# A two-layer trunk on one core: x also loaded by columns, and the first FFN's norm moved behind its first two column chunks

## The chip, the core and the metric

The kernel runs on one NeuronCore of a Trainium2 chip. Its engines work side by side, each through its own list of instructions in order: TensorE (PE; its weight loads are listed as PEld), VectorE (DVE), ScalarE (ACT), GpSimd (POOL), and SyncE (SP), which here only issues DMA transfers. They wait for each other through semaphores. TensorE takes its operands from SBUF and writes to PSUM, which has eight banks of 128x512 float32.

The metric is the device time of one execution in microseconds. Before the change it is 1176.08 us, the median of three runs (1176.0 to 1176.14).

## What is computed

Two layers, each of three sub-layers on the same 256x1024 stream x: a SwiGLU FFN with half a step, a token mixer (windowed attention beside a gated spatial unit), and a second FFN. Cut to what matters here:

```python
def rms_norm(x, g):
    x32 = x.astype(jnp.float32)
    y = x32 * lax.rsqrt(jnp.mean(x32 * x32, axis=-1, keepdims=True) + RMS_EPS)
    return (y * g.astype(jnp.float32)).astype(x.dtype)

def swiglu(x, w1, w2):
    g, u = jnp.split(x @ w1, 2, axis=-1)
    return (jax.nn.silu(g) * u) @ w2

for l in range(DEPTH):                       # DEPTH = 2
    h = rms_norm(x, ffn1_pre_g[l])
    x = x + 0.5 * rms_norm(swiglu(h, ffn1_w1[l], ffn1_w2[l]), ffn1_post_g[l])
    h = rms_norm(x, mix_pre_g[l])
    z = h @ w_in[l]
    ...                                      # attention, spatial gating, merge
    x = x + rms_norm(merged @ w_out[l], mix_post_g[l])
    h = rms_norm(x, ffn2_pre_g[l])
    x = x + 0.5 * rms_norm(swiglu(h, ffn2_w1[l], ffn2_w2[l]), ffn2_post_g[l])
```

x is 256x1024 (SEQ x D_MODEL), w1 is 1024x5632 (gate and value, 2816 columns each), w2 is 2816x1024. The part that changes is the very first FFN. Since the norm multiplies each token's row by one number, `rms_norm(x, g) @ w` equals `((x*g) @ w)` with each token's result multiplied by that number: the product can be taken first and scaled later.

## The kernel before

**Numbers.** Each product is made of three: every float32 operand is split in a high part (rounded to fp32r by ACT) and a low part (the rest, by DVE), and high x high, high x low and low x high are added up in PSUM. So each weight that is loaded costs one ACT cast (`Stream.high`, L143) and one DVE subtraction (`Stream.lower`, L152), and so does each activation.

**The stream of weights.** `Stream` holds all weights in units of 128x1024 float32 (512 KB) in the order in which they are used. SP loads a unit to one of four raw buffers (`RAW`); the load of unit u+4 is issued when DVE has made the low part of unit u (`low`, `lower`). `st.upto(n)` writes the casts and subtractions of all units below n into the lists of ACT and DVE at that place of the program. After `st.slip = True` each subtraction stands one unit behind its cast.

**The first FFN, first part.** The first 512 gate and 512 value columns (`FA` = 4 chunks of 128 of each) are computed token-major: for each of the two token tiles, 128 tokens of x are the stationary operand and 512 columns of weights the moving one. This takes eight units, 96 matmuls of 128x512, in `units(0)` to `units(7)` (helper L289). In the opening the input isn't normed yet. x comes in by rows, TensorE turns it (`transpose4`, L254, sixteen 128x128 transposes) and its gain is put on the weights or on x; the scale of the norm is put on the result in `first.finish` (L363, L364).

**The norm.** ACT squares and sums the rows (L214), DVE makes the inverse roots (L222 to L237) and a diagonal matrix from them (L269), TensorE spreads them over all partitions with a product with ones (L276), ACT copies that to SBUF (L278). DVE then multiplies the turned x with it (`norm`, L1141 and L1144), ACT casts and DVE subtracts (`high0`, `low0`, L1038, L1041). The result is `xt`, with high and low parts side by side for each of the eight 128-feature blocks k.

**The first FFN, second part.** The other 18 chunks of 128 gate and 128 value columns are computed feature-major in `FFN.middle`, chunks c = 4 to 21: the weights are stationary and `xt` moves. For one chunk `feature_pairs` (L319) issues 14 wide matmuls (512 columns: high and low part of x at once), 16 narrow ones (256 columns, low weights) and the two wide ones that were held back, gate and value each in a PSUM bank of its own. Then ACT copies (L680), DVE adds (L681), ACT takes the silu (L683), DVE multiplies gate by value (L684); then `st.upto` puts the casts and subtractions of two further units there, and the chunk's result is split for the second product (L206, L207). In the program `st.upto(8 + AHEAD)`, which covers the weights up to unit 14, and `first.finish` stand ahead of chunk 4's evacuation.

**What sets the order.** Everything is written out by hand; no scheduler moves an instruction. Each engine works through its list in the order of the program text, and the tile framework adds the waits. After the first FFN the kernel goes on through `project`, `Mix` and the others, which the change doesn't touch.

Of the kernel before, what the change touches and what calls it, by code (L numbers as in the profile page):

```python
# [54 lines left out]
WARM = (11, 6)  # L55
# [8 lines left out]
def trunk(ctx: ExitStack, tc: tile.TileContext, a: dict, out: bass.AP):  # L64
# [35 lines left out]
    class Stream:  # L100
        def __init__(self):
            self.src, self.where = [], []
            self.raw, self.split = {}, {}
            self.loaded = self.ready = 0
            self.free = RING
            self.rest = None
            self.slip = False
            self.gain = {}
# [14 lines left out]
        def first(self):  # L123

            self.raw[0] = new(rawp, [P, 1024], "raw")
            both = new(m8, [P, 2, 1024], "m8", F32R)
            self.split[0] = both[:, 0, :], both[:, 1, :]
            self.loaded = self.ready = 1
            for b in halves():
                nc.sync.dma_start(self.raw[0][:, b], self.src[0][:, b])  # L130
                yield
            for i in range(2):
                self.high(0, (i,))
                yield
                self.lower(0, (i,))
                yield
            del self.raw[0]
            self.load(1 + RAW)

        def high(self, u, which=(0, 1)):  # L140
            h = self.split[u][0]
            if u not in self.gain:
                nc.scalar.copy(h, self.raw[u])  # L143
                return
            for i in which:
                b = halves()[i]
                nc.scalar.activation(h[:, b], self.raw[u][:, b], AF.Copy, scale=self.gain[u][i])

        def lower(self, u, which=(0, 1)):
            h, lo = self.split[u]  # L150
            if u not in self.gain:
                nc.vector.tensor_tensor(out=lo, in0=self.raw[u], in1=f(h), op=ALU.subtract)  # L152
                return
            for i in which:
                b = halves()[i]
                nc.vector.scalar_tensor_tensor(out=lo[:, b], in0=self.raw[u][:, b], scalar=self.gain[u][i],
                                               in1=f(h[:, b]), op0=ALU.mult, op1=ALU.subtract)
# [25 lines left out]
        def low(self):  # L183

            if self.rest is not None:
                u = self.rest
                self.rest = None
                self.lower(u)
                del self.raw[u]
                self.load(u + 1 + RAW)  # L190
# [81 lines left out]
    def spread(dg):  # L272
# [4 lines left out]
        rb = new(t2, [P, n, P], "t2")  # L277
# [33 lines left out]
    def feature_pairs(os, us, both):  # L311
# [3 lines left out]
        wide = [[(o, st[u][0], flat(both[:, k]), k) for k in range(KD)] for o, u in zip(os, us)]  # L315
        narrow = [(o[:, 0:S], st[u][1], both[:, k, 0, :], k) for o, u in zip(os, us) for k in range(KD)]
# [334 lines left out]
    class FFN:  # L651
        def __init__(self, l, i, early=()):
            self.l, self.i = l, i
            w1, w2 = a[f"ffn{i}_w1"][l], a[f"ffn{i}_w2"][l]
            self.first = FirstFFN(l, i, early)
# [12 lines left out]
        def middle(self, xt, xth, xtl, turn1, early):  # L668
            for _ in range(2):
                self.into.append((new(m8, [P, 8, S], "m8", F32R), new(m8, [P, 8, S], "m8", F32R)))  # L670
            for c in range(FA, FC):
                o = [bank(), bank()]
                us = self.cols[(c - FA) * 2:(c - FA) * 2 + 2]
                feature_pairs(o, us, xt)
# [4 lines left out]
                for half in range(2):  # L679
                    nc.scalar.copy(y[:, half, :], o[half][:, S:2 * S])  # L680
                    nc.vector.tensor_tensor(out=y[:, half, :], in0=o[half][:, 0:S], in1=y[:, half, :], op=ALU.add)  # L681
                    if half == 0:
# [4 lines left out]
                split(hh, hl, s[:, S:2 * S])  # L687
                if c == FA + 2:
# [308 lines left out]
    def load_x(t, h):  # L997
        nc.sync.dma_start(xs[t][:, halves()[h]], a["x"][rows_of(t), halves()[h]])


    load_x(0, 0)
    begin = st.first()
    next(begin)
    load_x(1, 0)
    next(begin)
    st.load(2)
    load_x(0, 1)
    load_x(1, 1)
    st.load(RAW)

    for u in (0, 1, 4, 5):
        st.gain[u] = [g0[:, k:k + 1] for k in (u % 4 * 2, u % 4 * 2 + 1)]
# [15 lines left out]


    first = subs[0].first  # L1030
    xu = new(n8, [P, KD, S], "n8", F32R), new(n8, [P, KD, S], "n8", F32R)
    xg = [new(t4, [P, KD, P], "t4") for _ in range(NT)]

    def quarter0(t, h):
        return slice(None), slice(h * 4, h * 4 + 4), rows_of(t)

    def high0(x, t, h, src):
        nc.scalar.copy(x[0][quarter0(t, h)], src)  # L1038

    def low0(x, t, h, src):  # L1040
        nc.vector.tensor_tensor(out=x[1][quarter0(t, h)], in0=src, in1=f(x[0][quarter0(t, h)]), op=ALU.subtract)  # L1041

    one = []
    for t in range(NT):
        first.begin(t)
        one.append(first.steps(t, *xu)[3])

    def some(u, t, which):

        for k, i in which:  # L1050
            one[t](u // 4, u % 4 * 2 + k, (i,))
# [4 lines left out]
    def units(u):  # L1056

        for which in (SOON, LATE):
            for t in range(NT):
                some(u, t, which)  # L1060

    def warm(n):

        for _ in range(n):
            nc.tensor.transpose(cold[:, 0:P], ident, ident)  # L1065

    cold = bank()
# [3 lines left out]
    warm(WARM[0])  # L1071
    turned, src0 = {}, {}
    parts = [new(tiny2, [P, 2], "parts") for _ in range(NT)]

    def turn0(t, h):
# [170 lines left out]
```

## Time and profile before

| what | value |
|---|---|
| median of three runs | 1176.08 us (1176.0 to 1176.14) |
| the profiled execution: its time, its span | 1175.91 us, 1174.0 us |
| busy: PE, DVE, ACT, POOL | 1164.8, 842.6, 675.4, 58.9 us |
| instructions on PE | 6293 |
| HBM read over the span | 218.65 MB, 187 GB/s |

The time of an execution holds 1.9 us more than its span, which runs from the first instruction to the last. "Busy" counts an engine's instructions from start to end; matmuls overlap each other, so a lone 128x512 matmul is listed with 0.39 us while a row of them advances by some 0.23 us each. In a timeline row the first number is the start in us, the second the time from the first start to the last end of the merged instructions (xN), and a bracket tells how long the engine had been idle and what ended that.

### The profile page before, as it was taken

To read this page: it belongs to the slowest core of one execution; us is meant where nothing else is said; L and a number is where in the kernel's file an instruction comes from. 1 tells how busy PE (TensorE), PEld (TensorE's weight loads), DVE (VectorE), ACT (ScalarE), POOL (GpSimd) and SP (SyncE) were. 2 spreads that over 40 slices of the span, in tenths; PEclk is the share of its full clock that TensorE was granted. 3 is DMA by queue.
4 is the path that set the end of the run, shared out by engine and by line. 5 is a ranking of instruction groups with operands and counts; after the bars stand their busy time and mean duration, and the time that the engine had idled before them with its cause. 6 is when DMAs were issued, how large, how long until landed. Compare 5 with 4: busy or idle time off the path is not lost.

```text
span 1174.0 us, 16947 instructions
## 1 busy us (share of the span) xinstructions
PE 1164.8 (99%) x6293; PEld 1006.9 (86%) x6293; DVE 842.6 (72%) x1430; ACT 675.4 (58%) x1147; POOL 58.9 (5%) x43
## 2 busy tenths in 40 slices
PE   9999999999999999999999999999999999999997
PEld 7888888999888888888888888889988888888886
DVE  6767758877787867766676677589778787676752
ACT  6656644657775456555455665455577754555551
POOL 0000000001131000000000000000021220000000
PEclk9999999999999999999999999999999999999999
DMA  7576673645457346557635657745544662565560
GB/s 249 182 255 230 219 250 141 203 168 175 140 175 241 137 142 215 183 198 266 216 108 193 224 193 240 230 141 183 182 169 137 210 225 81 179 200 198 198 210 37
DMA packets 61427, 220.81 MB, mean 188 GB/s; under 512 B 7072, under 2 KB 7072, under 8 KB 61344
## 3 DMA queue, kind: packets, MB, share of 16 engines
q1 hardware_dynamic: 61056, 219.46, 56.1%
q8 instruction: 50, 0.82, 0.3%
q10 hardware_dynamic: 288, 0.27, 0.1%
q14 instruction: 33, 0.27, 0.1%
HBM read 218.65 MB, written 1.05 MB: 187 GB/s over the span
## 4 chain that ended last, share of the span: by engine, by line
PE 99%; ACT 0%; DVE 0%; issue 0%; DVEq 0%; POOL 0%; POOLq 0%
PE mm L289 51%; PE mm L319 34%; PE mm L296 3%; PE mm L297 3%; PE mm L298 3%; PE mm L254 1%; PE mm L803 1%; PE mm L767 1%; PE mm L766 1%; PE mm L736 1%; PE mm L816 0%; PE mm L815 0%; PE mm L1065 0%; PE mm L276 0%; ACT n L1038 0%; ACT t L1113 0%
## 5 line engine op out<-in xcount | busy, mean ns | idle before, releaser
L152 DVE TENSOR_TENSOR wl<-raw,wh 128x1024 fp32r<-128x1024 f32 x370 | 452.7, 1248 | 88.0 <-ACT wh L143 85.9
L143 ACT CAST wh<-raw 128x1024 fp32r<-128x1024 f32 x370 | 381.7, 1052 | 152.9 <-DMA raw<-in_ffn_w 71.4
L289 PE MATMUL mm<-wh,m 128*128 128x512 f32 x1088 | 341.7, 391 | 0.0
L319 PE MATMUL mm<-xt,wh 128*128 128x512 f32 x1152 | 276.6, 391 | 0.0
L319 PEld LDWEIGHTS mm<-xt,wh 128*128 128x128 f32 x1152 | 211.4, 188 | 40.7
L289 PEld LDWEIGHTS mm<-wh,m 128*128 128x128 f32 x1088 | 204.3, 188 | 42.1
L289 PE MATMUL mm<-wl,m 128*128 128x512 f32 x544 | 211.8, 389 | 0.0
L319 PEld LDWEIGHTS mm<-xt,wl 128*128 128x128 f32 x1152 | 147.7, 191 | 5.6
L319 PE MATMUL mm<-xt,wl 128*128 128x256 f32 x1152 | 149.4, 283 | 0.0
L289 PE MATMUL mm<-wh,xt 128*128 128x512 f32 (+1 forms) x480 | 144.1, 378 | 0.0
L681 DVE TENSOR_TENSOR t<-mm,t 128x256 f32<-128x256 f32 x144 | 61.0, 424 | 101.7 <-ACT t L680 101.7
L289 PEld LDWEIGHTS mm<-wl,m 128*128 128x128 f32 x544 | 102.2, 188 | 20.6
L680 ACT COPY t<-mm 128x256 f32<-128x256 f32 x144 | 52.4, 364 | 88.7 <-PE mm L319 88.7
L289 PEld LDWEIGHTS mm<-wh,xt 128*128 128x128 f32 x480 | 88.4, 188 | 16.0
L289 PE MATMUL mm<-wl,xt 128*128 128x512 f32 (+1 forms) x240 | 87.5, 375 | 0.0
L296 PE MATMUL mm<-xt,wh 128*128 128x256 f32 x256 | 73.3, 286 | 0.0
L298 PE MATMUL mm<-xt,wl 128*128 128x256 f32 x256 | 72.4, 283 | 0.0
L297 PE MATMUL mm<-xt,wh 128*128 128x256 f32 x256 | 72.4, 283 | 0.0
L683 ACT ACTIVATE t<-t 128x256 f32<-128x256 f32 x72 | 30.1, 418 | 46.3 <-DVE t L681 46.3
L289 PE MATMUL mm<-m,xt 128*128 128x512 f32 x216 | 54.5, 397 | 0.0
L289 PEld LDWEIGHTS mm<-wl,xt 128*128 128x128 f32 x240 | 45.2, 188 | 7.9
L794 POOL TENSOR_TENSOR t<-t,rd 128x1024 f32<-128x1024 f32 x12 | 26.1, 2171 | 505.8 <-DVE rd L793 488.2
(156 smaller groups left out, 1094.0 us busy)
## 6 DMA issues: line engine op xcount, KB each, us to landing
raw<-in_ffn_w SPq DMA_DIRECT2D x263, 512.0 KB, 4.5
raw<-in_w_in SPq DMA_DIRECT2D x84, 512.0 KB, 4.1
raw<-in_w_sgu_branch SPq DMA_DIRECT2D x16, 512.0 KB, 3.6
raw<-in_w_attn_branch SPq DMA_DIRECT2D x16, 512.0 KB, 3.8
raw<-in_w_out SPq DMA_DIRECT2D x16, 512.0 KB, 4.5
gain<-in_ffn_post_g SPq DMA_DIRECT2D x4, 512.0 KB, 6.4
gain<-in_ffn_pre_g SPq DMA_DIRECT2D x3, 512.0 KB, 6.7
x<-in_x SPq DMA_DIRECT2D x4, 256.0 KB, 4.9
```

The costliest lines, as they stand in the source:

```text
L143: nc.scalar.copy(h, self.raw[u])
L152: nc.vector.tensor_tensor(out=lo, in0=self.raw[u], in1=f(h), op=ALU.subtract)
L254: nc.tensor.transpose(ps[:, k, :], src[:, (c0 + k) * P:(c0 + k + 1) * P], ident)
L289: nc.tensor.matmul(o, every[i][0], every[i][1], start=start and i == 0, stop=stop and i == 2)
L296: nc.tensor.matmul(o, wh[:, ks], ah[:, k, :], start=(k == 0), stop=False)
L297: nc.tensor.matmul(o, wh[:, ks], al[:, k, :], start=False, stop=False)
L298: nc.tensor.matmul(o, wl[:, ks], ah[:, k, :], start=False, stop=(k == KD - 1))
L319: nc.tensor.matmul(out_, w[:, k * P:(k + 1) * P], x, start=(k == 0 and x.shape[1] == 2 * S), stop=(k == KD - 1 and x.shape[1] == 2 * S))
L680: nc.scalar.copy(y[:, half, :], o[half][:, S:2 * S])
L681: nc.vector.tensor_tensor(out=y[:, half, :], in0=o[half][:, 0:S], in1=y[:, half, :], op=ALU.add)
L683: nc.scalar.activation(y[:, 0, :], y[:, 0, :], AF.Silu)
L794: nc.gpsimd.tensor_tensor(out=p, in0=p, in1=rd[:, :nh].unsqueeze(2).to_broadcast([P, nh, nk]), op=ALU.mult)
```

## The change

x is loaded a second time, by columns: the host hands over `x_cols`, x transposed and grouped by pairs of 128-feature blocks, and SP loads it in six pieces between the first units (`load_cols`); x by rows (`xs`) is loaded after the unit-7 load. No transpose of x is left in the opening: `Opening.split` lets ACT multiply each 128-feature block with its gain and round it, and DVE make the low part. The weights are no longer multiplied by gains. Gate and value units alternate, so that both halves of the result go through the features in the same order. Fourteen warming transposes stand in one piece, where there were eleven and six.

The norm moves. The diagonal is made after all eight units' casts and subtractions, and its product with ones stands within unit 7. Chunks 4 and 5 (`SCALED` = 2) multiply the unnormed split x (`opening.raw`), and each adds two DVE multiplications with the spread scale to its evacuation (L673). `xt` itself is made in two halves: feature blocks 0 to 3 at the end of chunk 4's evacuation, 4 to 7 at the end of chunk 5's (`opening.norm`). Chunks 6 to 21 use `xt` as before.

```diff
-WARM = (11, 6)
+WARM = 14
+SCALED = 2
...
-        wide = [[(o, st[u][0], flat(both[:, k]), k) for k in range(KD)] for o, u in zip(os, us)]
+        wide = [[(o, st[u][0], flat(both(k)), k) for k in range(KD)] for o, u in zip(os, us)]
...
-        def __init__(self, l, i, early=()):
-            self.units = list(early)
-            for u in range(len(early), 8):
-                self.units.append(st.add(a[f"ffn{i}_w1"][l, u], "m8" if u < HOLD else "ring"))
+        def __init__(self, l, i, early, opening):
+            self.units = list(early) + [None] * (8 - len(early))
+            for j, u in enumerate([k + h * 4 for k in range(4) for h in range(2)] if opening else range(8)):
+                if self.units[u] is None:
+                    self.units[u] = st.add(a[f"ffn{i}_w1"][l, u], "m8" if j < HOLD else "ring")
...
+                raw = opening and c < FA + SCALED
-                feature_pairs(o, us, xt)
+                feature_pairs(o, us, opening.raw if raw else lambda k: xt[:, k])
...
                     nc.vector.tensor_tensor(out=y[:, half, :], in0=o[half][:, 0:S], in1=y[:, half, :], op=ALU.add)
+                    if raw:
+                        nc.vector.tensor_tensor(out=y[:, half, :], in0=y[:, half, :], in1=opening.scale(), op=ALU.mult)
...
                 split(hh, hl, s[:, S:2 * S])
+                if raw:
+                    opening.norm(range((c - FA) * KD // SCALED, (c - FA + 1) * KD // SCALED, 2))
...
+    def load_cols(k, n):
+        nc.sync.dma_start(x_cols(k, n), a["x_cols"][k // 2][:, k % 2:k % 2 + n, :])
+    st.open(2)
+    for i in range(2):
+        load_cols(i, 1)
+        st.load_half(0, i)
+    for i in range(2):
+        st.load_half(1, i)
+    load_cols(2, 2)
+    st.load(RAW)
+    load_cols(4, 2)
...
+        def split(self, k):
+            x, g, o = x_cols(k)[:, 0, :], g0[:, k:k + 1], self.raw(k)
+            nc.scalar.activation(o[:, 0, :], x, AF.Copy, scale=g)
+            nc.vector.scalar_tensor_tensor(out=o[:, 1, :], in0=x, scalar=g, in1=f(o[:, 0, :]), op0=ALU.mult,
+                                           op1=ALU.subtract)
...
+        def norm(self, chunks):
+            for k in chunks:
+                for j in range(k, k + 2):
+                    nc.vector.scalar_tensor_tensor(out=x_cols(j)[:, 0, :], in0=x_cols(j)[:, 0, :],
+                                                   scalar=g0[:, j:j + 1], in1=self.scale(), op0=ALU.mult, op1=ALU.mult)
+                nc.scalar.copy(xt[0][:, k:k + 2, :], x_cols(k, 2))
+            for k in chunks:
+                nc.vector.tensor_tensor(out=xt[1][:, k:k + 2, :], in0=x_cols(k, 2), in1=f(xt[0][:, k:k + 2, :]),
+                                        op=ALU.subtract)
...
+    for u in range(2):
+        for i, b in enumerate(halves()):
+            if u == 0:
+                opening.split(i)
+            st.high(u, b)
+            st.lower(u, b)
+            for j in (0, 2, 1):
+                some(u, ((i, j),))
+        st.release(u)
+        if u == 0:
+            load_cols(6, 2)
+    for u in range(2, 8):
+        if u % 2 == 0:
+            for k in (u, u + 1):
+                opening.split(k)
+        st.upto(u + 1)
+        if u == 3:
+            for t in range(NT):
+                nc.sync.dma_start(xs[t], a["x"][rows_of(t)])
+        if u < 7:
+            units(u)
...
     r01 = rsqrt([(total(p), 5) for p in parts])
     dg = diagonal(r01)
-    units(4)
-    st.upto(8)
-    rb = spread(dg)
-    units(5)
...
-    norm(0, 0)
-    norm(0, 1)
-    normed(0, 0)
     st.slip = True
-    st.upto(9)
-    norm(1, 0)
-    normed(0, 1)
-    norm(1, 1)
-    normed(1, 0)
-    normed(1, 1)
-    units(6)
-    units(7)
+    st.upto(10)
+    some(7, SOON)
+    opening.rb = spread(dg, gp, "gain")
+    some(7, LATE)
     st.upto(8 + AHEAD)
```

Three places show how the lists move. First DVE's list before the change, between the diagonal and the low parts of the weights of chunk 4 and later (`wl` are low parts of weight units, `xt` the normed input, `t_17` and `t_18` the turned x of the two token tiles, `t_74` the spread scale):

```order
L269 TENSOR_SCALAR t_66_331<-ident_99,ry_329 128x128
L152 TENSOR_TENSOR wl_347<-raw_242,wh_346 128x1024
L152 TENSOR_TENSOR wl_353<-raw_259,wh_352 128x1024
L1141 SCALAR_TENSOR_TENSOR t_17_139<-mm_161,g_4_106,t_74_360 128x128 x4
L1144 TENSOR_TENSOR t_17_139<-t_17_139,t_74_360 128x512
L1041 TENSOR_TENSOR xt_374<-t_17_139,xt_374 128x4x128
L1141 SCALAR_TENSOR_TENSOR t_18_140<-mm_178,g_4_106,t_74_360 128x128 x4
L1041 TENSOR_TENSOR xt_374<-t_17_139,xt_374 128x4x128
L1144 TENSOR_TENSOR t_18_140<-t_18_140,t_74_360 128x512
L1041 TENSOR_TENSOR xt_374<-t_18_140,xt_374 128x4x128 x2
L152 TENSOR_TENSOR wl_384<-raw_267,wh_383 128x1024
```

All of the norm stands ahead of the low part of unit 8 (`wl_384`). In the changed program the low part of unit 8 follows the diagonal at once, and DVE's list further on, from chunk 4's evacuation to the start of chunk 5's, reads (`mm_432` and `mm_433` are chunk 4's gate and value banks, `mm_497` chunk 5's gate bank, `gain_380` the spread scale, `t_5` the first four feature blocks of x):

```order
L671 TENSOR_TENSOR t_104_466<-mm_432,t_104_466 128x256
L673 TENSOR_TENSOR t_104_466<-t_104_466,gain_380 128x256
L671 TENSOR_TENSOR t_104_466<-mm_433,t_104_466 128x256
L673 TENSOR_TENSOR t_104_466<-t_104_466,gain_380 128x256
L676 TENSOR_TENSOR t_104_466<-t_104_466 128x256
L141 TENSOR_TENSOR wl_413<-raw_398,wh_412 128x1024
L141 TENSOR_TENSOR wl_476<-raw_404,wh_475 128x1024
L194 TENSOR_TENSOR m_93_419<-t_104_466,m_92_418 128x256
L1053 SCALAR_TENSOR_TENSOR t_5_108<-t_5_108,g_4_106,gain_380 128x256 x4
L1057 TENSOR_TENSOR xt_143<-t_5_108,xt_143 128x2x256 x2
L671 TENSOR_TENSOR t_113_531<-mm_497,t_113_531 128x256
```

The first half of the norm (L1053, L1057) now stands behind chunk 4's whole evacuation, and the second half in the same way behind chunk 5's. TensorE's list of the changed program from the end of chunk 5 into chunk 6 (`mm_562` is chunk 6's gate bank):

```order
L306 MATMUL mm_497<-n_19_142,wh_388 128x512
L306 MATMUL mm_498<-n_19_142,wh_394 128x512
L306 MATMUL mm_562<-xt_143,wh_400 128x512 [waits DVE_49]
L306 MATMUL mm_562<-xt_143,wh_400 128x512
L306 MATMUL mm_562<-xt_143,wh_400 128x512 [waits DVE_49]
L306 MATMUL mm_562<-xt_143,wh_400 128x512
L306 MATMUL mm_562<-xt_143,wh_400 128x512 [waits DVE_49]
L306 MATMUL mm_562<-xt_143,wh_400 128x512
L306 MATMUL mm_562<-xt_143,wh_400 128x512 [waits DVE_49]
```

Chunk 6 is the first to read `xt`, and its first seven matmuls wait for DVE at feature blocks 0, 2, 4 and 6; before the change these waits stood at chunk 4.

More of the change, by code (lines that the diff above doesn't have):

```diff
@@ L121, in load, with open, load_half, high @@
                 self.loaded += 1
[L123 to L149, printed above, removed]
[L150 to L157 removed]
+        def open(self, n):
+            for u in range(n):
+                self.raw[u] = new(rawp, [P, 1024], "raw")
+                both = new(m8, [P, 2, 1024], "m8", F32R)
+                self.split[u] = both[:, 0, :], both[:, 1, :]
+            self.loaded = self.ready = n
+        def load_half(self, u, i):
+            b = halves()[i]
+            nc.sync.dma_start(self.raw[u][:, b], self.src[u][:, b])
+        def high(self, u, b=slice(None)):
+            nc.scalar.copy(self.split[u][0][:, b], self.raw[u][:, b])
+        def lower(self, u, b=slice(None)):
+            h, lo = self.split[u]
+            nc.vector.tensor_tensor(out=lo[:, b], in0=self.raw[u][:, b], in1=f(h[:, b]), op=ALU.subtract)
+        def release(self, u):
+            del self.raw[u]
+            self.load(u + 1 + RAW)
         def upto(self, n, spare=0):
```

140 lines of the change are left out of this document (38 added, 102 removed).

## The prediction

> **What bounds the kernel now.** I read the page first, then three stretches of the span, then the timeline of the first 60 us engine by engine. The page's first line, and the table of stretches (length, then each engine's busy time with its instructions, the granted clock, the DMA share, GB/s):
>
> ```profile
> PE 1164.8 (99%) x6293; PEld 1006.9 (86%) x6293; DVE 842.6 (72%) x1430; ACT 675.4 (58%) x1147; POOL 58.9 (5%) x43
> ...
> 0.00:30.00 30.00, 27.87 (x123) 22.52 (x124) 20.35 (x50) 19.41 (x35) 2.58 (x12) 1.00 0.75 246
> 30.00:1160.00 1130.00, 1130.00 (x6143) 978.95 (x6142) 814.32 (x1359) 653.14 (x1104) 55.02 (x30) 1.00 0.56 188
> ```
>
> Between 30 and 1160 us PE is busy for 1130.00 of 1130 us. So TensorE is the bound and it has no idle time there in which a delay could be made good: whatever it gains in the opening, and whatever it loses before chunk 7, reaches the end whole. The question is therefore only when TensorE reaches the same matmul before and after; I take feature block 4 of chunk 6, behind the last wait that the change makes.
>
> In the opening, TensorE and its suppliers:
>
> ```profile
> 1.43 2.61 PE L1065 MATMUL mm<-ident 128*128 128x128 f32 x11 [1.43 <-POOL ident masks.py:199]
> 4.29 0.72 ACT L147 ACTIVATE m<-raw,g 128x512 fp32r<-128x512 f32 x1 [1.55 <-DMA raw<-in_ffn_w]
> 4.93 0.59 ACT L1038 CAST n<-mm 128x512 fp32r<-128x512 f32 x1
> 5.82 1.12 PE L289 MATMUL mm<-m,n 128*128 128x512 f32 x2
> 6.78 0.60 PE L254 MATMUL mm<-ident,x 128*128 128x128 f32 x4
> 10.78 1.03 PE L254 MATMUL mm<-ident,x 128*128 128x128 f32 x8
> 14.74 5.73 PE L289 MATMUL mm<-m,n 128*128 128x512 f32 x24 [0.19 <-ACT m L143]
> 20.31 1.52 PE L289 MATMUL mm<-wh,n 128*128 128x512 f32 x6
> 31.98 3.33 PE L319 MATMUL mm<-xt,wh 128*128 128x512 f32 x14
> 35.16 2.08 PE L319 MATMUL mm<-xt,wl 128*128 128x256 f32 x16
> 40.72 2.08 PE L319 MATMUL mm<-xt,wl 128*128 128x256 f32 x16
> 42.64 2.68 PE L319 MATMUL mm<-xt,wh 128*128 128x512 f32 x11
> ```
>
> The first real product stands at 5.82, chunk 4 starts at 31.98, and a chunk takes 40.72 - 35.16 = 5.56 us. The block at 42.64 begins with the last two matmuls of chunk 5, so chunk 6 starts at 43.1 and its feature block 4 at 44.0. A 128x512 matmul costs (20.31 - 14.74)/24 = 0.232 us.
>
> **Opening: what TensorE gains.** Of the transposes four stand ahead of 5.82; the other twelve (rows at 6.78 and 10.78) leave TensorE's path. The first product now waits for one column block of x (128 KB) and half a weight unit (256 KB) in place of 256 and 256 KB. The cast at 4.29 marks the landing; at the 344 GB/s below, 128 KB are 0.4 us, so it can start at 3.9 and, with 0.59 us for an unscaled cast (row at 4.93), the product at about 4.7 (bounds: 4.3 and, if the smaller pieces bring nothing, 5.1). From there 96 x 0.232 = 22.3, the spread product 0.3, and 1.0 us because the clock is still slow: the eleven transposes take 0.24 each, the eight at 10.78 0.13 each, so the first matmuls run at about half speed until about 6.7 us. Chunk 4 then starts at 4.7 + 22.3 + 0.3 + 1.0 = 28.3, which is **3.7 us earlier**. Suppliers keep up: a unit is 12 matmuls or 2.8 us for TensorE, and by the rows below 1.05 + 0.4 us for ACT, 1.2 + 0.4 for DVE, and 0.66 MB or 2.2 us at 298 GB/s for the DMA, x by columns included.
>
> **Chunks 4 and 5: what stands ahead of the norm.** Chunk 6 would now want `xt` at 28.3 + 2 x 5.56 = 39.4, its block 4 at 40.3. When does DVE deliver? The rows of today's chain:
>
> ```profile
> 0.00:5.00 5.00, 3.57 (x17) 3.57 (x18) 0.00 (x0) 2.19 (x4) 2.58 (x12) 1.00 0.61 188
> 5.00:10.00 5.00, 4.56 (x19) 3.15 (x18) 2.78 (x5) 3.10 (x8) 0.00 (x0) 1.00 1.01 344
> 10.00:15.00 5.00, 4.81 (x26) 3.77 (x25) 3.61 (x7) 4.01 (x9) 0.00 (x0) 1.00 0.89 298
> ...
> 18.00 0.61 ACT L214 ACTIVATE t<-x 128x512 f32<-128x512 f32 x1
> 20.69 0.22 DVE L244 SCALAR_TENSOR_TENSOR rv<-parts 128x1 f32<-128x1 f32 x2
> 23.03 2.36 DVE L152 TENSOR_TENSOR wl<-raw,wh 128x1024 fp32r<-128x1024 f32 x2
> 23.97 0.37 ACT L278 COPY t<-mm 128x256 f32<-128x256 f32 x1 [0.96 <-PE mm L276]
> 25.30 1.12 DVE L1141 SCALAR_TENSOR_TENSOR t<-mm,g,t 128x128 f32<-128x128 f32 x4
> ...
> 31.34 4.63 DVE L152 TENSOR_TENSOR wl<-raw,wh 128x1024 fp32r<-128x1024 f32 x4
> 32.63 26.36 SPq L120 DMA_DIRECT2D raw<-in_ffn_w  x12
> 36.19 1.05 ACT L143 CAST wh<-raw 128x1024 fp32r<-128x1024 f32 x1 [2.64 <-DMA raw<-in_ffn_w]
> 39.56 1.06 ACT L143 CAST wh<-raw 128x1024 fp32r<-128x1024 f32 x1 [0.25 <-DMA raw<-in_ffn_w]
> 40.64 1.28 ACT L363 ACT_TABLE_LOAD   x1
> 43.09 0.37 ACT L680 COPY t<-mm 128x256 f32<-128x256 f32 x1
> 43.98 0.42 DVE L681 TENSOR_TENSOR t<-mm,t 128x256 f32<-128x256 f32 x1
> ...
> 48.55 0.42 DVE L681 TENSOR_TENSOR t<-mm,t 128x256 f32<-128x256 f32 x1
> ```
>
> Chunk 4's matmuls are over at about 37.6 (the two held back stand at 37.07), yet its copy starts at 43.09: ACT's list has it behind the casts of units 8 to 14, and the last three wait for loads that SP may issue only when DVE has freed a raw buffer. Unit 8's low part starts at 31.34, SP issues unit 12 at 32.63, its cast comes at 36.19, unit 14's at 39.56, then the table of the silu at 40.64. Today this lag costs nothing, since nothing in chunks 5 and 6 waits for an evacuation. After the change chunk 6 does.
>
> The lag shrinks, but not enough. The norm leaves its place ahead of 31.34, so unit 8's low part follows the diagonal. That in turn waits for x by rows, which now lands last: eight units, x twice, 6.3 MB. The rows give 4.15 MB by 15.0 us; the other 2.15 MB take 6.2 to 7.2 us at 344 or 298 GB/s, so 21.7. Two squares of 0.61 follow (23.0), then the 2.34 us from DVE's total (20.69) to its next low part (23.03): 25.4. That is 5.9 us ahead of 31.34, and the table load comes at 40.64 - 5.9 = 34.7 (bounds: 33.5 if the data comes at 344 throughout, 40.64 if nothing is gained). As today, chunk 4's first addition follows 3.34 us later (43.98 - 40.64): 38.1.
>
> **The norm behind two evacuations.** From chunk 4's first addition to chunk 5's DVE needs 48.55 - 43.98 = 4.57 us today: additions, gating, two low parts of weights, the chunk's split. New in it are two 256-wide scalings, each waiting for the addition before it and waited for by the silu or the gating (0.42 each as at 43.98, and a little for the wait, 0.9 in all); four 256-wide scalar-tensor products of the norm; and two 512-wide subtractions. The four products have no row of their size. The nearest are below and above:
>
> ```profile
> 9.27 2.08 DVE L156 SCALAR_TENSOR_TENSOR m<-raw,g,m 128x512 fp32r<-128x512 f32 x3 [0.54 <-ACT m L147]
> ...
> 53.12 1.28 DVE L207 TENSOR_TENSOR m<-mm,m 128x512 fp32r<-128x512 f32 x2
> ```
>
> 0.28 for 128 columns (row at 25.30), 0.69 for 512: between 1.1 and 2.8 for four, by width 1.6. The two subtractions advance by 0.6 each (row at 53.12), 1.2, and I put 0.2 on the ACT cast between products and subtractions. A period is 4.57 + 0.9 + 3.0 = 8.5 us (8.0 to 9.7). Nothing of it overlaps: DVE's list is serial, and the second half of the norm stands behind chunk 5's evacuation, which stands behind the first half. Feature block 4 is ready at 38.1 + 2 x 8.5 - 0.6 (the last subtraction comes after it) = 54.5; block 6 comes 0.6 later, of which two matmuls cover 0.46. Against 44.0 today that is 10.5 + 0.1 = **10.6 us later**; the 3.7 us from the opening are already in it, since DVE, and no longer TensorE, sets this time.
>
> **The clock after the stall.** TensorE stands still from about 39.4 until block 0 (about 46), does four matmuls, and stands again until 54.5. The end of today's span shows what a pause does; its last matmul and the stretches after it:
>
> ```profile
> 1166.55 0.39 PE L289 MATMUL mm<-wh,m 128*128 128x512 f32 x1
> ...
> 1168.00:1170.00 2.00, 0.00 (x0) 0.00 (x0) 1.82 (x7) 0.00 (x0) 0.00 (x0) 1.00 0.03 10
> 1170.00:1172.00 2.00, 0.00 (x0) 0.00 (x0) 0.87 (x2) 0.00 (x0) 0.00 (x0) 0.67 0.46 170
> 1172.00:1174.00 2.00, 0.00 (x0) 0.00 (x0) 0.00 (x0) 0.00 (x0) 0.00 (x0) 0.50 0.25 92
> ```
>
> After 1166.94 nothing runs, and the granted clock falls from 1.00 to 0.50 within 1170 to 1172, 3 to 5 us later. Both pauses are longer. In the opening the slow rate lasted from 1.43 to about 6.7, 5.3 us of work; the same here, at half speed, loses **2.6 us** (bounds 0 and 2.6). The Trainium skill (TensorE: Matmul & The Clock Gate, "What's actually happening") puts both switches at a free-running window of about 3.4 us; by that the slow work lasts 3.4 to 6.8 us and an estimate of the loss is 1.7 to 3.4 us, which would make the sum 12.3 to 14.0. The tail's 0.67 and 0.50 agree with the fall; no run here shows the return after a pause.
>
> At no cost: the four alternating units, the gains that leave the weights, the scale's place in a `gain` buffer (read for the last time before chunk 6), and x staying longer in `t4` and `n8`, which nothing claims before the mixer. Under the stall DVE, ACT and the loads run ahead, so no later wait is added; but by the table of stretches no later wait was there to be saved either.
>
> **Sum.** 10.6 + 2.6 = 13.2 us. Span 1174.0 + 13.2 = 1187.2; the profiled execution took 1175.91, 1.9 more than its span and 0.2 under the median. On the median: 1176.08 + 13.2 = **1189.3 us**.
>
> **Rivals.**
> - *The stall without the clock* (0.13): four matmuls between the pauses, or another phase of the throttle, keep it at 1.00. 1176.08 + 10.6 = 1186.7. Against it: both pauses exceed what the tail needed.
> - *DVE catches up early* (0.10): ACT reaches chunk 4's copy as soon as its matmuls end, 28.3 + 5.6 = 33.9, addition at 34.8; block 4 at 34.8 + 17.0 - 0.6 = 51.2. 7.3 + 2.6 gives 1186.0, and 1182.9 with DVE idle even at chunk 5's end (block 4 at 48.1). The last is the floor of a stall: one period after 39.4. Against it: the loads of units 12 to 14.
> - *The lag stays* (0.07): x by rows lands so late, or the loads so slowly, that the table load stays at 40.64. Block 4 at 60.4, 16.5 + 2.6, 1195.2.
> - *The norm is hidden; faster* (0.03). The scale is on SBUF 1.3 us after the diagonal, at 26.7, and the norm is 6 us of DVE; taken at once it would be done at 32.7, ahead of 39.4, and the opening's 3.7 us would stay: 1172.4. It decides from the point where block 4 comes before 44.0, which by the sums above means a table load before 24.2. Against it are DVE's list, where both halves stand behind evacuations, and x by rows landing at 21.7.
> - *A draw* (0.01), if a late opening met that early chain.
>
> **How the numbers follow.** Forecast 0.66. This kernel's runs tell a change of 0.2% (2.4 us) from none. Faster 0.03, same 0.01, slower 0.96. The range 1183.5 to 1194.5 takes in the clock's bounds (1186.7), a period of 8.0 to 9.7 (1188.3 to 1191.7), a table load 3 us either way, and most of the early case; outside are the draw, the faster case, half of the early one and the late one, some 0.16.
>
> **What would show it.** Right: chunk 4's first matmul near 28; two idle times of some 6 to 8 us on PE ahead of `mm<-xt,wh`, released by DVE's low part of `xt`; the silu's table load near 34 to 35; two DVE periods of 8 to 9 us; a clock of 0.50 in part of 45 to 60; all later stages moved by one amount. Wrong: PE busy throughout from 5 to 60 us (the norm is hidden), one short stall only (DVE had caught up), or a clock of 1.00 behind the stall.

## The result, and the profile after

The changed kernel takes 1191.53 us, the median of four runs (1190.94 to 1192.13). The kernel before, on the same chip, takes 1176.04 us (1175.65 to 1176.14). The ratio is 1.0131 [1.0119, 1.0143]: slower by 1.3%, or 15.5 us, where 13.2 were forecast. The profiled execution took 1190.94 us with a span of 1189.1, so the spans differ by 15.1 us.

The page of the changed kernel gives TensorE 0.3 us less busy time than before, so the time that came is time in which TensorE stands still. Most of that stands in one row, at the feature-major product, and DVE's low part of `xt` ends it:

```profile
PE 1164.5 (98%) x6274; PEld 1005.5 (85%) x6274; DVE 846.5 (71%) x1433; ACT 675.5 (57%) x1145; POOL 58.0 (5%) x43
...
L306 PE MATMUL mm<-xt,wh 128*128 128x512 f32 x1120 | 271.9, 394 | 13.2 <-DVE xt L1057 13.2
```

TensorE's timeline around the change. The first five rows below are of the changed kernel, the row after them is the one of the kernel before that answers to the last (line 254 there is line 241 here: the first transposes behind chunk 6).

```profile
28.80 3.35 PE L306 MATMUL mm<-n,wh 128*128 128x512 f32 x14
...
39.47 0.63 PE L306 MATMUL mm<-n,wh 128*128 128x512 f32 x2
46.95 2.08 PE L306 MATMUL mm<-xt,wh 128*128 128x512 f32 x4 [6.86 <-DVE xt L1057]
...
55.40 4.19 PE L306 MATMUL mm<-xt,wh 128*128 128x512 f32 x10 [6.37 <-DVE xt L1057]
...
61.80 1.03 PE L241 MATMUL mm<-ident,t 128*128 128x128 f32 x8
```

```profile
48.67 1.03 PE L254 MATMUL mm<-ident,t 128*128 128x128 f32 x8
```

Chunk 4 starts at 28.80, 3.2 us earlier than before (31.98). Chunks 4 and 5 run through, and at 40.09 TensorE stops. It does four matmuls at 46.95, with feature blocks 0 to 3, stops again, and goes on at 55.40. Before, feature block 4 stood at 44.0, so here the delay is 11.4 us; at the transposes it is 61.80 - 48.67 = 13.1.

What TensorE waits for, in the changed kernel's lists of DVE and (one row, the table load) ACT:

```profile
26.26 2.35 DVE L141 TENSOR_TENSOR wl<-raw,wh 128x1024 fp32r<-128x1024 f32 x2
...
39.15 0.42 DVE L671 TENSOR_TENSOR t<-mm,t 128x256 f32<-128x256 f32 x1
...
42.03 2.35 DVE L141 TENSOR_TENSOR wl<-raw,wh 128x1024 fp32r<-128x1024 f32 x2
...
44.63 1.66 DVE L1053 SCALAR_TENSOR_TENSOR t<-t,g,gain 128x256 f32<-128x256 f32 x4
46.22 1.46 DVE L1057 TENSOR_TENSOR xt<-t,xt 128x512 fp32r<-128x512 f32 x2
47.59 0.42 DVE L671 TENSOR_TENSOR t<-mm,t 128x256 f32<-128x256 f32 x1
...
54.66 1.46 DVE L1057 TENSOR_TENSOR xt<-t,xt 128x512 fp32r<-128x512 f32 x2
```

```profile
35.80 1.28 ACT L352 ACT_TABLE_LOAD   x1
```

The four products and two subtractions of half a norm take 44.63 to 47.68, 3 us; they begin only when chunk 4's additions, gating, two weight subtractions and split are done, which started at 39.15. Chunk 5's first addition comes at 47.59, so a period is 8.44 us, and the second half ends behind a second period.

The table of stretches (length, then busy time of PE, PEld, DVE, ACT and POOL with their instructions, the granted clock, the DMA share, GB/s) has borders set where the granted clock changes:

```profile
30.00:45.00 15.00, 10.10 (x60) 8.66 (x58) 10.10 (x15) 8.84 (x12) 0.00 (x0) 1.00 0.57 191
45.30:58.90 13.60, 5.58 (x12) 3.82 (x13) 9.81 (x19) 5.62 (x10) 0.00 (x0) 0.50 0.39 142
59.00:65.00 6.00, 6.00 (x40) 5.36 (x39) 1.62 (x3) 1.64 (x4) 0.00 (x0) 1.00 0.01 3
65.00:1175.00 1110.00, 1108.23 (x6019) 959.85 (x6018) 797.34 (x1333) 635.93 (x1079) 54.16 (x30) 1.00 0.56 187
```

The clock is at 0.50 from 45.3 to 58.9. Of that, the work of 55.40 to 58.9 counts, 3.5 us at half speed. The last row holds a surprise: between 65 and 1175 us TensorE is busy for 1108.23 of 1110.00 us, so 1.77 us are missing where nothing was missing before. The view of waits for the stretch from 70 to 1175 us names them as one wait in the second layer's attention (total, times, longest):

```profile
PE mm L760 <- ACT n L929: 1.8, 1, 1.8
```

The account of the 15.1 us: 11.4 (feature block 4) + 1.7 (from there to the transposes) + 1.8 (attention) = 14.9; 0.2 isn't traced.

### The profile page after: what moved, and what is told of

The parts are those of the page before. It is cut to its first block, busy times and chain, and to the rows that moved or that the text cites. A ratio compares the mean times of both kernels' runs of the same rounds, so it can differ in the third digit from the quotient of the medians.

```text
span 1189.1 us, 16919 instructions
## 1 busy us (share of the span) xinstructions
PE 1164.5 (98%) x6274; PEld 1005.5 (85%) x6274; DVE 846.5 (71%) x1433; ACT 675.5 (57%) x1145; POOL 58.0 (5%) x43
## 4 chain that ended last, share of the span: by engine, by line
PE 95%; DVE 2%; DMA 1%; ACT 1%; issue 0%; SPq 0%; DVEq 0%; ACTq 0%
PE mm L276 50%; PE mm L306 33%; PE mm L283 3%; PE mm L284 3%; PE mm L285 3%; PE mm L241 1%; DMA raw<-in_ffn_w 1%; PE mm L797 1%; PE mm L760 1%; PE mm L761 1%; PE mm L730 1%; DVE wl L141 0%; PE mm L810 0%; PE mm L809 0%; DVE t L1053 0%
## 5 line engine op out<-in xcount | busy, mean ns | idle before, releaser
L306 PE MATMUL mm<-xt,wh 128*128 128x512 f32 x1120 | 271.9, 394 | 13.2 <-DVE xt L1057 13.2
L306 PEld LDWEIGHTS mm<-xt,wh 128*128 128x128 f32 x1120 | 206.9, 190 | 54.5 <-DVE xt L1057 14.9
L306 PEld LDWEIGHTS mm<-xt,wl 128*128 128x128 f32 x1120 | 143.6, 191 | 5.5
L306 PE MATMUL mm<-xt,wl 128*128 128x256 f32 x1120 | 145.3, 283 | 0.0
L285 PE MATMUL mm<-xt,wl 128*128 128x256 f32 x256 | 72.4, 283 | 0.0
L276 PE MATMUL mm<-m,xt 128*128 128x512 f32 x216 | 54.5, 397 | 0.0
```

The source lines that it names most:

```text
L276: nc.tensor.matmul(o, every[i][0], every[i][1], start=start and i == 0, stop=stop and i == 2)
L285: nc.tensor.matmul(o, wl[:, ks], ah[:, k, :], start=False, stop=(k == KD - 1))
L306: nc.tensor.matmul(out_, w[:, k * P:(k + 1) * P], x, start=(k == 0 and x.shape[1] == 2 * S), stop=(k == KD - 1 and x.shape[1] == 2 * S))
```

## The experiments

**Once more, and the third wait.** The same program was run again, since 1.8 us of a wait so far from the change could be an accident of one execution.

> The changed kernel once more, beside the others on the same chip. By the profile of the changed kernel its span holds, against before: 11.4 us at feature block 4 of chunk 6 (two idle times of TensorE, 6.9 and 6.4 us), 1.8 us from 3.5 us of matmuls at a clock of 0.50, and 1.8 us from an idle time at 902 us, in the second layer's attention, that nobody forecast. If that third idle time belongs to the changed kernel, it is there again at the same place and the time is 1191 to 1192; if it is an accident of one execution, it is gone or elsewhere, and the time of this profile is near 1189.5.

1191.29 us (1190.32 to 1192.25), ratio 1.013 [1.0115, 1.0144]. The wait is there again, of the same length. The clock is low for 17 us instead of 13.6, and feature block 4 comes 0.9 us later, since DVE's first addition of chunk 4 stands at 40.08 instead of 39.15:

```profile
PE mm L760 <- ACT n L929: 1.8, 1, 1.8
```

```profile
43.95:60.95 17.00, 6.70 (x15) 4.69 (x16) 12.09 (x23) 5.62 (x10) 0.00 (x0) 0.50 0.36 124
...
56.33 4.64 PE L306 MATMUL mm<-xt,wh 128*128 128x512 f32 x10 [6.37 <-DVE xt L1057]
...
63.24 1.04 PE L241 MATMUL mm<-ident,t 128*128 128x128 f32 x8
```

So the third wait belongs to this program. Its chain is read in the timeline of the changed kernel between 891 and 903 us:

```profile
891.64 1.89 POOL L788 TENSOR_TENSOR t<-t,rd 128x1024 f32<-128x1024 f32 x1 [8.44 <-DVE rd L787]
891.72 2.89 DVE L141 TENSOR_TENSOR wl<-raw,wh 128x1024 fp32r<-128x1024 f32 x1 [0.25 <-issue]
...
894.54 1.40 DVE L823 TENSOR_TENSOR t<-mm,t 64x512 f32<-64x512 f32 x2
...
898.53 0.41 ACT L780 ACTIVATE t<-t,nm 128x128 f32<-128x128 f32 x1 [0.98 <-DVE nm L771]
...
901.73 0.56 ACT L929 COPY n<-mm 128x512 f32<-128x512 f32 x1
...
902.34 0.39 PE L760 MATMUL mm<-kth,m 128*128 128x256 f32 x1 [1.77 <-ACT n L929]
```

The same place in the kernel before:

```profile
878.23 1.21 DVE L152 TENSOR_TENSOR wl<-raw,wh 128x1024 fp32r<-128x1024 f32 x1
...
878.48 2.71 POOL L794 TENSOR_TENSOR t<-t,rd 128x1024 f32<-128x1024 f32 x1 [8.44 <-DVE rd L793]
```

A weight subtraction takes 1.21 us on DVE, and this one took 2.89. It began 0.08 us after a GpSimd multiplication and ended 1.08 us after that one's end (893.53). Before, DVE was first by 0.25 us: its subtraction took 1.21 and GpSimd's multiplication 2.71 instead of 1.89. In both pairs the one that began first took its usual time, and the other ended 1.1 to 1.8 us behind it. The Trainium skill (SBUF — State Buffer, "Who interferes with whom") states such a lock, which goes to the one that starts first, for a VectorE instruction with two SBUF inputs against a GpSimd one that reads SBUF; the two pairs of rows agree with it. Behind the late subtraction stand DVE's additions (894.54), ACT's exponentials (898.53 to 901.6), the copy L929 and TensorE. The seven profiles of the experiments fit: the wait of 1.76 to 1.77 us is in the four where GpSimd is first, and in none of the two where DVE is (the seventh has GpSimd's part taken out, below). Why DVE is 0.3 us later at this place in some programs, the traces do not tell: the row says "issue", which means that nothing visible held it.

**The multiplication on the other engine.** To test that chain, the second layer's multiplication was moved from GpSimd to DVE.

```diff
-            nc.gpsimd.tensor_tensor(out=p, in0=p, in1=rd[:, :nh].unsqueeze(2).to_broadcast([P, nh, nk]),
+            (nc.vector if l else nc.gpsimd).tensor_tensor(out=p, in0=p, in1=rd[:, :nh].unsqueeze(2).to_broadcast([P, nh, nk]),
```

> The changed kernel with the six multiplications of the second layer's attention that GpSimd does (t<-t,rd, about 2 us each) moved to VectorE. In the profile the idle time at 902 us follows a VectorE subtraction of 2.89 us in place of 1.22, which starts 0.08 us after such a GpSimd multiplication and ends after it. Theory: the two engines get in each other's way; then the long subtraction and the idle time are gone, 1189.8 (six multiplications of 1.2 us more on VectorE are hidden). Rival: the idle time comes from ACT or a load and stays, 1191.5; or VectorE's added work opens idle times of its own, above 1192.

1191.06 us (1189.94 to 1191.78), ratio 1.0127 [1.0113, 1.0141]; the 1189.8 expected was not reached, and the time alone decides nothing, since it overlaps with the repeat's. In its trace no weight subtraction at that place takes 2.9 us (the longest is 1.23), and the wait has shrunk:

```profile
PE mm L760 <- ACT n L929: 1.0, 1, 1.0
```

The remaining 1.0 us goes with the edit's own cost: DVE now does the multiplication itself, 1.22 us, ahead of the same chain. That GpSimd's multiplication made the 1.8 us is thus supported by the lengths of the instructions, not by the time. A version that removes the wait without a new one was not made.

**The clock apart from the stall.** 60 and 66 transposes into PSUM banks that nobody reads fill TensorE's two pauses, so that the clock has no reason to fall, while DVE's list stays as it is.

```diff
-        for out_, w, x, k in todo:
+        for n_, (out_, w, x, k) in enumerate(todo):
+            if n_ in idle:
+                spare = bank()
+                for _ in range(idle[n_]):
+                    nc.tensor.transpose(spare[:, 0:P], ident, ident)
...
+                              {0: 60, 4: 66} if opening and c == FA + 2 else {})
```

> The changed kernel with 60 idle transposes on TensorE ahead of chunk 6 and 66 ahead of its feature block 4 (6.5 and 7.1 us at 0.108 us each), into PSUM banks that nobody reads: they fill the two idle times and make nothing else later. If the pauses cost their length and the clock besides, the clock stays at 1.00 and the kernel is 1.8 us faster than the changed one, near 1189.7, with chunk 6's block 4 still at 55.4. If the clock costs nothing, the same 1191.5; if the transposes themselves delay something, slower.

1189.76 us (1189.17 to 1191.32), ratio 1.0119 [1.0105, 1.0133], 1.5 to 1.8 us under the unedited program. Its TensorE timeline and one stretch:

```profile
39.53 6.71 PE L309 MATMUL mm<-ident 128*128 128x128 f32 x60
...
47.70 7.37 PE L309 MATMUL mm<-ident 128*128 128x128 f32 x66
...
54.82 2.87 PE L310 MATMUL mm<-xt,wh 128*128 128x512 f32 x10
...
59.91 1.04 PE L241 MATMUL mm<-ident,t 128*128 128x128 f32 x8
```

```profile
45.00:60.00 15.00, 14.80 (x111) 13.07 (x110) 9.51 (x18) 5.58 (x10) 0.00 (x0) 1.00 0.36 121
```

The two medians differ by no more than the runs of one program do, so the reading rests on the rows. The clock stays at 1.00, and from feature block 4 to the transposes it takes 59.91 - 54.82 = 5.1 us, where the changed kernel needs 61.80 - 55.40 = 6.4. The slow clock therefore costs 1.3 us in that execution, half of the 2.6 forecast; in the repeat it is 63.24 - 56.33 = 6.9, a cost of 1.8. Block 4 didn't stay at 55.4, as was expected here, but came at 54.82. That isn't the clock's doing: DVE's whole chain was earlier in this execution (chunk 4's first addition at 38.55, ahead of any pause). In the four profiles whose DVE list is the same up to here, block 4 came between 54.82 and 56.33, while the period was 8.44 us in each. Block 6's wait is in the 5.1: the ten matmuls take 2.87 us where 9 x 0.232 + 0.39 = 2.5 would do, so it is 0.4 and not 0.1; at the slow clock the two matmuls ahead of it take twice as long and cover more of it.

**The norm ahead of the evacuations.** The last rival of the prediction held that a norm taken at once after the diagonal would be done before chunk 6. Here both halves stand behind the low parts of units 8 to 10 and ahead of everything else on DVE; the first two chunks still run ahead of the norm and are scaled later.

```diff
-                if raw:
-                    opening.norm(range((c - FA) * KD // SCALED, (c - FA + 1) * KD // SCALED, 2))
...
     some(7, LATE)
+    st.upto(12)
+    opening.norm(range(0, KD, 2))
     st.upto(8 + AHEAD)
```

> The changed kernel with both halves of the norm moved ahead of the two evacuations: behind the low parts of units 8 to 11 and ahead of the casts of units 12 to 14. All else stays, the two unscaled chunks, the scalings and both loads of x too. Theory (the place in VectorE's list is the whole loss): the low parts of units 8 to 11 end at 31.3, the norm takes 6.2 us, 37.5, ahead of the 39.9 at which chunk 6 wants it; no idle time at chunk 6, no slow clock, and the opening's gain (chunk 4 at 28.8 against 31.98) stays: 1172.5 to 1173.5, and 1.8 more if an idle time in the attention comes. Rival 1 (VectorE has too much work there, wherever the norm stands): units 12 to 14 are subtracted 6 us later and chunk 6 or 7 waits for them, 1176 to 1183. Rival 2 (the second load of x delays the weights): still above 1185.

1172.55 us (1172.25 to 1172.98, seven runs), ratio 0.9969 [0.9958, 0.998]: faster than both kernels, by 3.6 us than the one before. DVE's and TensorE's rows, and two stretches behind the opening:

```profile
26.66 3.62 DVE L141 TENSOR_TENSOR wl<-raw,wh 128x1024 fp32r<-128x1024 f32 x3
30.20 3.25 DVE L1051 SCALAR_TENSOR_TENSOR t<-t,g,gain 128x256 f32<-128x256 f32 x8
33.37 2.48 DVE L1055 TENSOR_TENSOR xt<-t,xt 128x512 fp32r<-128x512 f32 x4
...
40.50 0.41 DVE L671 TENSOR_TENSOR t<-mm,t 128x256 f32<-128x256 f32 x1
```

```profile
28.87 3.34 PE L306 MATMUL mm<-n,wh 128*128 128x512 f32 x14
...
39.99 3.35 PE L306 MATMUL mm<-xt,wh 128*128 128x512 f32 x14
...
45.56 1.03 PE L241 MATMUL mm<-ident,t 128*128 128x128 f32 x8
```

```profile
30.00:60.00 30.00, 30.00 (x175) 26.51 (x174) 26.75 (x46) 20.73 (x35) 0.00 (x0) 1.00 0.56 203
60.00:1150.00 1090.00, 1089.71 (x5923) 944.27 (x5922) 789.11 (x1324) 629.70 (x1068) 55.26 (x30) 1.00 0.57 189
```

The expectation counted the low part of unit 11 ahead of the norm too. Since each subtraction stands one unit behind its cast here, it stands behind the norm (the first row has three), and the norm begins at 30.20 instead of 31.3. It takes DVE to 35.85. Chunk 6 wants it at 39.99 and starts there without a pause, the clock stays at 1.00, and the transposes come at 45.56, 3.1 us earlier than before. From 60 to 1150 us TensorE lacks 0.3 us, one wait at another place; the wait in attention is gone, and GpSimd comes second there again. Chunk 4's first addition is now at 40.50, 1.35 us later than in the changed kernel, and that costs nothing, since no matmul waits for it. What made the change slow is the place of the norm in DVE's list; the other parts, taken together, gain. The gain in the two profiled spans is 1174.0 - 1171.3 = 2.7 us, the 3.1 less that 0.3; the 3.6 of the medians holds some difference between executions besides.

**Half of the way: all of the norm behind chunk 4 alone.**

```diff
-                if raw:
-                    opening.norm(range((c - FA) * KD // SCALED, (c - FA + 1) * KD // SCALED, 2))
+                if raw and c == FA:
+                    opening.norm(range(0, KD, 2))
```

> The changed kernel with the whole norm at the end of chunk 4's evacuation, none behind chunk 5's. Theory (block 4 pays for two evacuations, one of them 5.4 us): in the changed kernel chunk 4's first addition stands at 39.15 and its evacuation ends at 44.63; eight products are 3.3 us, so block 0 is ready at 48.6 and, at 0.6 us for each subtraction, block 4 at 49.8. Against 44.0 before, 5.8, one pause of 8.7 us in place of two, the clock falls all the same, 1.8: 1183.7, or 1185.5 with the idle time in the attention. Rival (chunk 6 waits for its weights or for PSUM banks anyway): 1189 or more.

1185.01 us (1184.77 to 1185.82), ratio 1.0071 [1.0056, 1.0086]. One pause instead of two, and 6.5 us of the loss given back:

```profile
48.80 5.14 PE L306 MATMUL mm<-xt,wh 128*128 128x512 f32 x14 [8.39 <-DVE xt L1057]
...
56.16 1.04 PE L241 MATMUL mm<-ident,t 128*128 128x128 f32 x8
```

Chunk 6 takes 56.16 - 48.80 = 7.4 us where it takes 45.56 - 39.99 = 5.6 at full clock: the slow clock costs 1.8 here. The wait in attention is there again in this program.

**The other half: each half of the norm ahead of its chunk's evacuation.** The same two halves, moved up by one evacuation without being joined.

```diff
+                if raw:
+                    opening.norm(range((c - FA) * KD // SCALED, (c - FA + 1) * KD // SCALED, 2))
                 s = new(t2, [P, 512], "t2")
...
                 split(hh, hl, s[:, S:2 * S])
-                if raw:
-                    opening.norm(range((c - FA) * KD // SCALED, (c - FA + 1) * KD // SCALED, 2))
```

> The changed kernel with each half of the norm ahead of the evacuation behind which it stands (blocks 0 to 3 ahead of chunk 4's copies and additions, 4 to 7 ahead of chunk 5's). Theory: block 0 is ready at 39.15 + 1.66 + 0.7 = 41.5, then chunk 4's evacuation, 5.5, then block 4 at about 50.0; 6.0 later than before, one short pause of some 1.3 us and one of 7.7, the clock falls in the second, 1.8: 1184, or 1185.7 with the idle time in the attention. Rival (the second evacuation's length doesn't count, only when DVE starts): block 4 still near 55, 1190 or more.

1187.27 us (1185.05 to 1187.71), ratio 1.009 [1.0073, 1.0107]. The median is above the 1184 to 1185.7 expected. The profiled run is the lowest, 1185.05, and shows the stalls that were expected, a short pause ahead of block 0 and a long one ahead of block 4:

```profile
41.23 1.51 PE L306 MATMUL mm<-xt,wh 128*128 128x512 f32 x4 [1.33 <-DVE xt L1057]
...
49.68 4.08 PE L306 MATMUL mm<-xt,wh 128*128 128x512 f32 x10 [6.94 <-DVE xt L1057]
```

The median of the runs is 2.2 us above that one, and no trace shows why; a later block 4 and a longer slow clock, as in the repeat above, would fit. The mean granted clock of the other three runs, 0.992 to 0.994 against 0.995, points that way. The order holds: with one evacuation less ahead of the second half, block 4 comes 5.7 us earlier (49.68 against 55.40), and the medians are 4.3 us apart.

**The opening alone.** The new opening is kept, but all chunks use the normed `xt`, as they did before the change. The norm stands still earlier than in the norm-ahead version, at once behind the low part of unit 8.

```diff
-                raw = opening and c < FA + SCALED
+                raw = False
...
     some(7, LATE)
+    opening.norm(range(0, KD, 2))
     st.upto(8 + AHEAD)
```

> The opening of the changed kernel alone: x by columns, alternating units, no transposes; but no unscaled chunks. The norm stands behind the low part of unit 9 and chunks 4 to 21 all use xt. Theory (the opening's lead can only be kept if TensorE has something to do that needs no norm): by the rows of the changed kernel the low parts of units 8 and 9 end at 28.6, eight products 3.3, the first subtraction 0.7, block 0 at 32.6 and block 6 at 34.4; chunk 4 could start at 28.8 and starts at 32.6, against 31.98 before: 1176.7 to 1177.5, up to 1.8 more if the clock falls in a pause of 3.8 us. Rival (the lead stays without them): 1173.

1177.45 us (1176.85 to 1179.27, ten runs), ratio 1.0011 [1.0001, 1.002]: no gain, and 1.2 us above the median of the kernel before beside it, 1176.22. Its first chunk, and the stretches around it:

```profile
31.46 5.04 PE L306 MATMUL mm<-xt,wh 128*128 128x512 f32 x14 [2.97 <-DVE xt L1055]
```

```profile
28.00:31.40 3.40, 0.49 (x3) 0.06 (x1) 3.40 (x10) 2.42 (x5) 0.00 (x0) 1.00 0.51 154
31.50:34.85 3.35, 3.35 (x8) 2.69 (x9) 3.35 (x5) 2.79 (x3) 0.00 (x0) 0.50 0.00 0
```

TensorE waits 2.97 us for the norm and gets back to work at 31.46, half a microsecond before the kernel before does. (The 32.6 expected had unit 9's low part, 1.2 us, ahead of the norm; as above, it stands behind.) But the pause has let the clock fall, and the 14 matmuls take 5.04 us instead of 3.34, 1.7 more: 1.7 - 0.5 is the 1.2 us. So in these versions the faster opening is worth something only with two chunks that don't wait for the norm: together the two give the 3.6 us of the norm-ahead version, the opening by itself none, and both with the norm late lose 15.5. Whether the opening alone would gain with the clock kept up through its pause was not tried.

## Why the prediction was right, and where it was not

The sign, the place and the mechanism were right: TensorE stands still ahead of chunk 6 because both halves of the norm are behind evacuations on DVE. By its own steps:

| step | forecast | measured |
|---|---|---|
| chunk 4's first matmul | 28.3 us | 28.80 |
| table load of the silu | 34.7 | 35.80 |
| chunk 4's first addition | 38.1 | 39.15 |
| DVE's period | 8.5 | 8.44 |
| feature block 4 of chunk 6 | 54.5 | 55.40 |
| its delay | 10.5 | 11.4 |
| clock and block 6, to the transposes | 2.6 + 0.1 | 1.7 |
| later waits | 0 | 1.8 |
| sum | 13.2 | 15.1 in the span, 15.5 in the medians |

*Opening.* The gain came as 3.2 us instead of 3.7. In TensorE's timeline of the changed kernel:

```profile
4.69 1.66 PE L276 MATMUL mm<-m,n 128*128 128x512 f32 x6
...
6.98 4.39 PE L276 MATMUL mm<-m,n 128*128 128x512 f32 x18 [0.64 <-ACT m L137]
...
11.86 5.76 PE L276 MATMUL mm<-m,n 128*128 128x512 f32 x24 [0.48 <-ACT m L137]
```

The first product stands at 4.69 (4.7 forecast). The six first matmuls advance at nearly the full rate, so the 1.0 us put down for a slow clock wasn't lost. "Suppliers keep up" failed by about as much: two pauses, 0.64 and 0.48 us, wait for casts of weights, ahead of which ACT had waited for loads (1.03 us for x's second column block, 0.35 us for a weight unit). This differs between executions: in the repeat the first 24 matmuls take 6.61 us without a pause, 0.9 more than at the full rate, so there the clock was slow at first, and one pause of 1.46 us follows. In the six profiles with the same lists up to here chunk 4 starts between 28.40 and 29.55. The norm-ahead version shows that what is gained in the opening reaches the end: 3.1 us at chunk 4, at chunk 6 and at the transposes.

*The lag of the evacuations.* The table load was 1.1 us later than forecast. The step that was mis-sized is "two squares of 0.61 follow": all four squares stand behind the landing of x by rows, in ACT's timeline from 21.32 to

```profile
23.25 0.61 ACT L201 ACTIVATE t<-x 128x512 f32<-128x512 f32 x1
```

so the diagonal and unit 8's low part came 0.9 later (26.26, not 25.4); the first token tile of x had landed at 21.3, where both were forecast for 21.7. From there to the table load it took 9.54 us, 0.24 more than before.

*The period* was right, and so were its parts: 5.48 us from chunk 4's first addition to the norm (5.47 forecast), 2.96 for half the norm (3.0), in it the four products 1.66 (1.6 forecast, between bounds of 1.1 and 2.8).

*The clock* was mis-sized. The forecast let TensorE work 5.3 us at half speed, as in the opening before the change; it was 3.5 in the changed kernel's profile, and 1.3 us of loss by the version that is kept warm. The 5.3 was one case of a time that varies: with the same two stalls it was 4.7 us in the repeat and 2.9 in the version with the moved multiplication. The Trainium skill (TensorE: Matmul & The Clock Gate, "What's actually happening") gives a free-running window of about 3.4 us for both switches, from which the prediction estimated 3.4 to 6.8 us of slow work. The 3.5 and the 4.7 lie in that estimate, the 2.9 below it.

*"No later wait is added"* was wrong. The prediction argued from TensorE's full rows and from engines that run ahead; it did not ask who begins first where DVE and GpSimd meet. The 1.8 us in the second layer's attention is a real part of this program's time, seen in both of its profiles at the same length and in three of its variants, but it depends on 0.3 us at one place, in code that the change leaves alone.

The two errors of the sum, 1.0 too much for the clock and 1.8 too little for later waits, offset each other in part, which is luck; with 0.9 from the lag, 0.2 not traced and 0.4 from how the profiled runs stand to their medians, that makes 13.2 into 15.5.

*The rivals.* "The stall without the clock", "DVE catches up early" and "the lag stays" are excluded by the rows above: a clock of 0.50 behind the stall, a first addition of chunk 4 at 39.15 where the rival had 34.8, a table load 4.8 us earlier than before. "The norm is hidden" was false of this program, and its price, 1172.4 us, is close to what the norm-ahead version measured, 1172.55; in part by chance, since it counted 3.7 us for the opening, of which the profile shows 3.1.

## What to carry to other kernels

Work that is put off until "later" lands in an engine's list behind whatever stands there; before a product is set to run ahead of a norm, find the place in VectorE's list where the norm itself is then done, and the first matmul that wants it. Two chunks of cover, 11.1 us of matmuls, were enough for 5.7 us of norm when it stood first, and not when two evacuations of 5.5 us stood in front of it. A long pause of TensorE costs more than its length: behind the last one, of 2.97 to 8.39 us in these versions, the slow clock took another 1.0 to 1.8 us, while a pause of 1.33 us left the clock at 1.00.

## What the runs showed of the hardware

**The clock moves in steps of 3.41 us.** In the profiled runs the stretch at 0.50 lasted 3.41 us (opening alone), 6.83 (norm behind chunk 4, and each half ahead of its evacuation), 13.65 (the changed kernel, and with the multiplication moved) and 17.07 (the repeat): 1, 2, 4 and 5 times 3.41. The rows also show that a pause shorter than a step is enough: in the opening-alone version the pause is 2.97 us, the step up to 31.4 holds 0.49 us of TensorE's work, and the clock falls at its end. In the norm-behind-chunk-4 version it falls only at 45.6, 5.2 us after TensorE stopped, so the delay depends on where in a step the pause begins. The return depends on it too: after the last pause TensorE worked 2.9 us at half speed with the multiplication moved (55.65 to 58.56), 3.5 in the changed kernel and 4.7 in the repeat (56.33 to 61.00). In the repeat the step from 54.2 to 57.6, which held only the first 1.3 us of this work, didn't bring the clock back, the full one behind it did. The Trainium skill (TensorE: Matmul & The Clock Gate, "What's actually happening") gives a free-running window of about 3.4 us and asks for an idle one; the steps agree with the length, and the opening-alone row shows that a window with some work in it counts as idle too.

**A GpSimd multiplication that began 0.08 us ahead of a VectorE subtraction made that 1.7 us longer** (2.89 instead of 1.21), and by way of softmax cost TensorE 1.8 us, 850 us behind the changed part of the program.
